# Hybrid encoder layer on one core: other buffers for the latent branch's operands, POOL for the preparation's copies

## The chip, the cores and the metric

The kernel runs on one core of one Trainium2 chip. The metric is device time in microseconds (us), the median of several executions; the profile is of one execution. The engines are TensorE (PE; its weight loads are listed as PEld), VectorE (DVE), ScalarE (ACT), GpSimd (POOL) and the queue of SyncE (SP), which issues most transfers.

## The reference, cut to what matters

One encoder layer in float32 over 2 x 256 tokens of width 1024. After an RMS norm, one wide projection feeds three branches, each with a silu gate and its own projection (br) to 1024 columns; the three are gated, added, projected by w_out and added to x, and a last norm follows.

```python
o_fwd = _gdn_chunked(q, k, v, g[:, :, 0], beta[:, :, 0])          # branch A, 8 heads, both directions
o_gdn = _rmsnorm(o_fwd + o_bwd, gdn_norm_gain) * silu(z_gdn)
o_mla = _blocked_attention(q_full, k_full, v_mla, scale) * silu(z_mla)   # branch B, "latent"
o_mem = (softmax(qx @ km.T) @ vm) * silu(z_mem)                   # branch C, memory tokens
merged = (gates[0] * (o_gdn @ w_br_gdn) + gates[1] * (o_mla @ w_br_mla)
          + gates[2] * (o_mem @ w_br_mem))
return x + merged @ w_out
```

Branch A is a gated delta rule. Within blocks of 32 tokens it needs the inverse of a triangular matrix (I + L) for every head, direction and block.

## The kernel before, in words

All large products are done in three passes of rounded operands (hi x hi, lo x hi, hi x lo). `gemm` (L231) does one tile of 128 outputs by 512 tokens: 8 blocks of the input x 3 passes = 24 matmuls, which the planner counts at 0.234 us each. `weight` (L196) loads the tile's 512 KB of weights on SP into one of two buffers, rounds them on ScalarE (wh, L207) and takes the rest on VectorE (wl, L211). `split` (L216) does the same for an operand: hi on ScalarE (L219), lo on VectorE (L223). Activations on chip are tiles of 128 x 512.

There are three stages. `front` does the memory and latent attention and writes the latent branch's 8 gated operands to DRAM (d_xa). `middle` does the 8 heads of branch A. `back` does the projection of branch A (bg, needs all heads' normed outputs xg; head 7's operand is used in the last 3 of a tile's 24 matmuls), then the output.

**The order in the middle.** `weave` (L1515) writes PE's order by hand from a plan. Several chains of small steps each yield (PE time, delay until their next step); in between, `products` takes single matmuls from a list of filling (`self.fill`, L1365 to L1372): projections, gates, and at its end the memory branch (`branch_mem`, a gate tile g and 12 products be for each of 8 tiles) and the latent branch's projection (`branch`, tiles bm). The first entry that `can` (L1502) allows is taken; where none is allowed, the plan's clock jumps. Only PE's order is fixed so. The other engines' and queues' instructions are put in order by a scheduler that goes by priority and its own estimate of readiness; `issue_after` keeps an instruction behind another on its engine.

**A head's chain.** Its decays e and values are loaded (L912 to L919; head h waits until head h-3 has given its output), its keys split into kh, kl (L959, L961) and multiplied (kk, L971). A solve (`gdn_solve`, two lanes: even and odd heads) follows, in links about 6.5 planned us apart: p (L1022, reads t32), yp (L1047, reads y32), then twice u (L1078), xs (L1088), us (L1097), with x (L1068) between the two rounds. ScalarE copies the results (u2 L1080, ub L1083 and L1100). The output o (L1121) reads ub; so (L1137) sums squares 11 planned us later (13 for head 7), and after a trip through DRAM the normed operand xg is split (L1153, L219, L223).

**The preparation** (`gdn_prep`, once for heads 0 to 3 and once for 4 to 7) inverts all blocks at once on VectorE: 31 steps of two instructions, then ScalarE reorders tt into ts (L873), VectorE transposes ts and tt into o1 and o2 (L876, L878), and ScalarE copies parts of them into t32 (four of 32 partitions, L891) and y32 (L895, L899).

**The latent operands** are read back from d_xa in six parts (`load_xa`, L1570) into tiles that something else has given up, and split (`split_xa`, L1581). Tags are shared storage: na is a head's masked keys (3 buffers), y0 and y1 the two lanes' block matrices, ub a head's result (2), y32 as above (2). A split is placed at the earliest XAT = 14 planned us after its load, except for part 5. Tile 7 of `branch_mem` is held until part 5 has been asked for (L1511), and no `branch` starts until all eight operands are split (L1513).

Of the kernel before, what the change touches and what calls it, by code (L numbers as in the profile page):

```python
# [7 lines left out]
F32 = mybir.dt.float32  # L8
F32R = mybir.dt.float32r
AF = mybir.ActivationFunctionType  # L10
# [3 lines left out]
P = 128  # L14
# [4 lines left out]
XAT = 14.0  # L19
# [136 lines left out]
class Layer:  # L156
# [74 lines left out]
    def gemm(self, src, nk, xs, name, m=P, ps=None):  # L231

        nc = self.nc
        hi, lo = self.weight(src, nk * m, name)
        ps = self.ps_gm("gm_" + name) if ps is None else ps
        n = 0
        order = [(p, k) for p in ((hi, 0), (hi, 1), (lo, 0)) for k in range(nk)]
        last = {"bm": 6, "bg": 7, "qm": 4}.get(name[:2])
        if last:

            order.sort(key=lambda o: o[1] >= last)
        for (a, j), k in order:
            nc.tensor.matmul(ps[:m], a[:, k * m:(k + 1) * m], xs[k][j],  # L243
                             start=n == 0, stop=n == 3 * nk - 1)
            n += 1
            yield 0.234
        return ps
# [526 lines left out]
    def gdn_prep(self, g):  # L774
# [4 lines left out]
        nc, c = self.nc, self.c  # L779
# [33 lines left out]
        with self.tc.high_priority(offset=0 if g else 900):  # L813
            for h in range(4):
                for s in range(2):
                    for cc in range(2):
                        w = h * 4 + s * 2 + cc
                        for a in range(4):
                            t = slice(cc * P + 32 * a, cc * P + 32 * a + 32)
# [28 lines left out]
        for d in range(2):  # L848
            t = self.tb(f"nd{g}{d}").rearrange("p (w i) -> p w i", i=32)
# [14 lines left out]
        tt, tms = self.tt, self.pb.tile([P, 4, 256], F32, tag="blk", bufs=3, name=f"tm{g}")  # L864
# [5 lines left out]
            nc.vector.tensor_tensor(tt[:, m:, 0:m], tt[:, m:, 0:m], t3, op=ALU.add)  # L870
            yield 0.0, 1.2
        ts = self.pb.tile([P, 32, 32], F32, tag="blk", bufs=3, name=f"ts{g}")
        nc.scalar.activation(ts, tt.rearrange("p r c -> p c r"), AF.Copy)  # L873
        yield 0.0, 4.0
        o1 = self.pb.tile([P, 32, 32], F32, tag="blk", bufs=3, name=f"o1{g}")
        nc.vector.transpose(out=o1.rearrange("p i j -> p (i j)"), in_=ts.rearrange("p i j -> p (i j)"))  # L876
        o2 = self.pb.tile([P, 32, 32], F32, tag="blk", bufs=3, name=f"o2{g}")
# [6 lines left out]
        t32 = self.pg.tile([P, 16, 32], F32, tag="t32", bufs=2, name=f"t32{g}")  # L884

        y32 = self.pg.tile([P, 32, 32], F32, tag="y32", bufs=2, name=f"y32{g}")
        for a in range(4):
            r = slice(32 * a, 32 * a + 32)
            d = a % 2
            with self.tc.issue_after(self.wround):  # L890
                nc.scalar.activation(t32[r], (o2 if d else o1)[r, :, 16 * d:16 * d + 16].rearrange("p i u -> p u i"),  # L891
                                     AF.Copy)
            yield 0.0, 4.5 if g else 2.8
        with self.tc.issue_after(self.wround):
            nc.scalar.activation(y32[:, 0:16], o2[:, :, 0:16].rearrange("p i u -> p u i"), AF.Copy)  # L895
        yield 0.0, 4.5 if g else 2.8
        for q in range(2):
            with self.tc.issue_after(self.wround):
                nc.scalar.activation(y32[:, 16 + q:32:2], o1[:, :, 17 - q:32:2].rearrange("p i u -> p u i"), AF.Copy)  # L899
            yield 0.0, 4.5 if g else 2.8  # L900
        self.ready[g] = self.now + 4
        return t32, y32, cc

# [598 lines left out]
    def can(self, f, *a):  # L1502

        if f == self.load_xa:
            return (3 in self.ub and self.pr[1], 5 in self.ub and 7 in self.hd, 6 in self.ub and 7 in self.hd,
                    7 in self.started, self.out > 6 and 7 in self.started, 7 in self.ub)[a[0]]
        if f == self.split_x:
            return self.now > self.xe_at
        if f == self.split_xa:
            return self.now > self.xa_at.get(a[0], 1e9)  # L1510
        if f == self.branch_mem and a[0] == 7:  # L1511
            return 5 in self.xa_raw
        return f != self.branch or None not in self.xa  # L1513

    def weave(self, *chains):  # L1515
# [53 lines left out]

    def load_xa(self, part):  # L1570

        lo, tags = ((0, ("y32",)), (1, ("na",)), (2, ("na", "y0")), (4, ("y32",)), (5, ("ub",)), (6, ("na", "y1")))[part]
        ts = [self.pg.tile([P, 2, 512], F32R, tag=t, bufs={"na": 3, "y0": 1, "y1": 1}.get(t, 2), name=f"xa{f}")
              for f, t in enumerate(tags, lo)]
        for f, t in enumerate(ts, lo):
            self.nc.sync.dma_start(t[:, 1].bitcast(F32), self.d_xa[:, f])
        self.xa_at[part] = self.now + XAT if part < 5 else self.now
        self.xa_raw[part] = ts, lo
        yield 0.0

    def split_xa(self, part):  # L1581
        ts, lo = self.xa_raw[part]
        with self.tc.issue_after(self.wround):
            for f, t in enumerate(ts, lo):
                self.xa[f] = t[:, 0], t[:, 1]
                self.split(t[:, 1].bitcast(F32), t[:, 0], t[:, 1], 0.5)
        yield 0.0


# [22 lines left out]
```

## Time and profile before

| | us |
|---|---|
| median of 3 executions (878.02 to 880.48) | 880.07 |
| the profiled execution | 877.71 |
| its span, first to last instruction | 875.9 |
| PE busy in it | 855.2 (98%) |
| VectorE, ScalarE, POOL busy | 564.1, 472.5, 120.1 |

Busy time says how long an engine had an instruction, not how late it got it. PE is nearly always busy, so what there is to read are the few stretches where it is not, and the granted clock there (1.00 is TensorE's full speed). A bracket behind an instruction gives the idle time before it on its engine and what ended it.

### The profile page before, as it was taken

How to read it: one execution, taken by the hardware profiler on the slowest of the kernel's cores; microseconds unless marked ns; L12 is line 12 of the kernel's file. 1: busy time of each engine (PE TensorE's matmuls, PEld its weight loads, DVE VectorE, ACT ScalarE, POOL GpSimd, SP SyncE). 2: the span in 40 equal slices, each digit the busy share in tenths (PEclk: the TensorE clock that was granted, in tenths of full speed). 3: DMA queues.
4: the chain of work that ended last, by engine and by line, in shares of the span. 5: the costliest groups of instructions: out<-in, count | busy, mean ns of one | idle time of the engine just before them, and what ended most of it. 6: DMA issues, size and time to landing. Idle time of an engine off the chain costs nothing.

```text
span 875.9 us, 13248 instructions
## 1 busy us (share of the span) xinstructions
PE 855.2 (98%) x4854; PEld 705.2 (81%) x4854; DVE 564.1 (64%) x1013; ACT 472.5 (54%) x915; POOL 120.1 (14%) x119
## 2 busy tenths in 40 slices
PE   8999998999999999999999989999999989999997
PEld 7878887878888888887888878888888878888886
DVE  7776458866989765547889967584654443335643
ACT  7655455554654565676675677666464532222232
POOL 0200111000100000141101211311110001432121
PEclk9999999999999999999999999999999989999999
DMA  9322212442235324373323455535533435465332
GB/s 330 127 91 79 90 67 64 133 140 76 83 112 160 120 90 147 115 216 109 105 90 126 127 156 168 160 111 159 169 123 95 164 123 201 161 221 183 120 97 96
DMA packets 50865, 116.10 MB, mean 133 GB/s; under 512 B 7152, under 2 KB 12656, under 8 KB 50800
## 3 DMA queue, kind: packets, MB, share of 16 engines
q1 hardware_dynamic: 44896, 104.51, 37.4%
q10 hardware_dynamic: 5904, 10.75, 3.5%
q8 instruction: 38, 0.62, 0.3%
q14 instruction: 27, 0.22, 0.1%
HBM read 95.09 MB, written 16.99 MB: 128 GB/s over the span
## 4 chain that ended last, share of the span: by engine, by line
PE 92%; ACT 3%; DVE 2%; DMA 2%; issue 1%; POOL 0%; POOLq 0%; DVEq 0%; ACTq 0%; SPq 0%
PE gm_g L243 16%; PE gm_qkv L243 14%; PE gm_z L243 7%; PE gm_bm L243 5%; PE gm_bg L243 5%; PE gm_za L243 5%; PE y L1256 4%; PE vm L396 3%; PE o L1121 3%; PE gm_be L243 3%; PE gm_qm L243 3%; PE gm_km L243 3%; PE kk L971 2%; PE s_a L305 2%; PE gm_cq L243 2%; PE gm_qn L243 2%
## 5 line engine op out<-in xcount | busy, mean ns | idle before, releaser
L742 DVE SCALAR_TENSOR_TENSOR kq<-cz,prm,kq 128x510 f32<-128x510 f32 (+1 forms) x64 | 47.8, 747 | 13.3 <-ACT kq L735 12.6
L243 PE MATMUL gm_g<-hh,wh_g 128*128 128x512 f32 x192 | 52.0, 405 | 0.6 <-ACT cz L733 0.6
L243 PE MATMUL gm_g<-hh,wl_g 128*128 128x512 f32 x192 | 51.8, 400 | 0.0
L243 PE MATMUL gm_qkv<-hh,wl_qkv 128*128 128x512 f32 x192 | 51.6, 399 | 0.0
L243 PE MATMUL gm_g<-hl,wh_g 128*128 128x512 f32 x192 | 50.4, 398 | 0.0
L243 PE MATMUL gm_qkv<-hh,wh_qkv 128*128 128x512 f32 x192 | 50.4, 399 | 0.0
L243 PE MATMUL gm_qkv<-hl,wh_qkv 128*128 128x512 f32 x192 | 49.7, 396 | 0.0
L211 DVE TENSOR_TENSOR wl_qkv<-wr_qkv,wh_qkv 128x1024 fp32r<-128x1024 f32 x24 | 30.0, 1249 | 26.7 <-ACT wh_qkv L207 12.2
L211 DVE TENSOR_TENSOR wl_g<-wr_g,wh_g 128x1024 fp32r<-128x1024 f32 x24 | 29.5, 1229 | 21.6 <-ACT wh_g L207 11.2
L243 PEld LDWEIGHTS gm_qkv<-hl,wh_qkv 128*128 128x128 f32 x192 | 35.8, 188 | 8.3
L243 PEld LDWEIGHTS gm_g<-hh,wh_g 128*128 128x128 f32 x192 | 35.4, 191 | 8.4 <-ACT cz L733 1.0
L243 PEld LDWEIGHTS gm_g<-hl,wh_g 128*128 128x128 f32 x192 | 35.5, 188 | 7.9
L243 PEld LDWEIGHTS gm_g<-hh,wl_g 128*128 128x128 f32 x192 | 35.2, 188 | 7.4
L243 PEld LDWEIGHTS gm_qkv<-hh,wl_qkv 128*128 128x128 f32 x192 | 35.2, 188 | 7.4
L243 PEld LDWEIGHTS gm_qkv<-hh,wh_qkv 128*128 128x128 f32 x192 | 35.1, 188 | 7.5
L1256 PE MATMUL y<-wh_wo,mh 128*128 128x512 f32 (+1 forms) x144 | 40.0, 370 | 0.0
L1226 POOL TENSOR_TENSOR mg<-mg,lg 128x512 f32<-128x512 f32 x16 | 28.0, 1750 | 57.2 <-DVE lg L1225 52.7
L207 ACT ACTIVATE wh_qkv<-wr_qkv 128x1024 fp32r<-128x1024 f32 x24 | 25.3, 1055 | 19.1 <-PE gm_qkv L243 4.7
L207 ACT ACTIVATE wh_g<-wr_g 128x1024 fp32r<-128x1024 f32 x24 | 25.3, 1056 | 17.1 <-PE gm_g L243 6.0
L961 POOL TENSOR_TENSOR kl<-kq,kh 128x512 fp32r<-128x512 f32 x16 | 22.1, 1386 | 81.3 <-ACT kh L959 81.2
L243 PE MATMUL gm_bm<-xa,wh_bm 128*128 128x512 f32 x128 | 32.4, 395 | 0.0
L243 PE MATMUL gm_bg<-xg,wh_bg 128*128 128x512 f32 x128 | 32.4, 394 | 0.0
(433 smaller groups left out, 2200.8 us busy)
## 6 DMA issues: line engine op xcount, KB each, us to landing
wr_qkv<-in_w_dram SPq DMA_DIRECT2D x24, 512.0 KB
wr_g<-in_w_dram SPq DMA_DIRECT2D x24, 512.0 KB
e<-d_r SPq DMA_DIRECT2D x64, 96.0 KB
wr_z<-in_w_dram SPq DMA_DIRECT2D x12, 512.0 KB
wr_za<-in_w_dram SPq DMA_DIRECT2D x8, 512.0 KB
d_g<-gt_g ACTq DMA_DIRECT2D x16, 256.0 KB
wr_bm<-in_w_dram SPq DMA_DIRECT2D x8, 512.0 KB
lg<-d_g SPq DMA_DIRECT2D x16, 256.0 KB
```

What stands on the lines that cost most here:

```text
L207: self.wround = nc.scalar.activation(hi[:, :n], raw[:, :n], AF.Copy).ins
L211: d = eng.tensor_tensor(lo[:, :n], raw[:, :n], hi[:, :n].bitcast(F32), op=ALU.subtract)
L243: nc.tensor.matmul(ps[:m], a[:, k * m:(k + 1) * m], xs[k][j], start=n == 0, stop=n == 3 * nk - 1)
L305: nc.tensor.matmul(sp[:, qb * 256:(qb + 1) * 256], a, b, start=j == 0, stop=j == n - 1)
L396: nc.tensor.matmul(vps[tb], ms[k][a][:, t], b[:, :512], start=k == 0 and i == 0, stop=k == 7 and i == 2)
L742: nc.vector.scalar_tensor_tensor(ys, zs, self.cw[:, f, m:m + 1], ys, ALU.mult, ALU.add)
L961: nc.gpsimd.tensor_tensor(lo, src, hi.bitcast(F32), op=ALU.subtract)
L971: nc.tensor.matmul(ps, a[:, k], b, start=i == 0, stop=i == 2)
L1121: nc.tensor.matmul(out, ub[:, d, s, cp], rhs, start=n == 0, stop=n == 3)
L1226: nc.gpsimd.tensor_tensor(self.merged[d], self.merged[d], gt, op=ALU.add)
L1256: nc.tensor.matmul(ps, xs[2 * j + q][a][:, t], b[:, q * 512 + c0:q * 512 + c1], start=j == 0 and n == 0, stop=j == 3 and n == 5)
```

## The change

The transfers of the latent operands go to other tiles: operands 3 and 4 to the keys' tiles (kh and kl), 5 to y32, 6 to two tiles of decays (e), 7 to two of t32; 0, 1 and 2 as before to y32 and na. Parts are grouped anew, the conditions under which the plan asks for them are others, all parts are split 14 planned us after their load at the earliest, and tile 7 of the memory branch is no longer held. In a bm tile the products with operands 5 to 7 instead of 6 and 7 come last. The preparation's eight copies of each pass are made by POOL, without being kept behind a weight's rounding, and the plan counts 2.8 us after each of the last seven in both passes (before: 4.5 in the second).

```diff
--- before.py
+++ after.py
@@ -235,7 +235,7 @@
         ps = self.ps_gm("gm_" + name) if ps is None else ps
         n = 0
         order = [(p, k) for p in ((hi, 0), (hi, 1), (lo, 0)) for k in range(nk)]
-        last = {"bm": 6, "bg": 7, "qm": 4}.get(name[:2])
+        last = {"bm": 5, "bg": 7, "qm": 4}.get(name[:2])
         if last:
 
             order.sort(key=lambda o: o[1] >= last)
@@ -870,7 +870,7 @@
             nc.vector.tensor_tensor(tt[:, m:, 0:m], tt[:, m:, 0:m], t3, op=ALU.add)
             yield 0.0, 1.2
         ts = self.pb.tile([P, 32, 32], F32, tag="blk", bufs=3, name=f"ts{g}")
-        nc.scalar.activation(ts, tt.rearrange("p r c -> p c r"), AF.Copy)
+        nc.gpsimd.tensor_copy(out=ts, in_=tt.rearrange("p r c -> p c r"))
         yield 0.0, 4.0
         o1 = self.pb.tile([P, 32, 32], F32, tag="blk", bufs=3, name=f"o1{g}")
         nc.vector.transpose(out=o1.rearrange("p i j -> p (i j)"), in_=ts.rearrange("p i j -> p (i j)"))
@@ -887,17 +887,13 @@
         for a in range(4):
             r = slice(32 * a, 32 * a + 32)
             d = a % 2
-            with self.tc.issue_after(self.wround):
-                nc.scalar.activation(t32[r], (o2 if d else o1)[r, :, 16 * d:16 * d + 16].rearrange("p i u -> p u i"),
-                                     AF.Copy)
-            yield 0.0, 4.5 if g else 2.8
-        with self.tc.issue_after(self.wround):
-            nc.scalar.activation(y32[:, 0:16], o2[:, :, 0:16].rearrange("p i u -> p u i"), AF.Copy)
-        yield 0.0, 4.5 if g else 2.8
+            nc.gpsimd.tensor_copy(out=t32[r], in_=(o2 if d else o1)[r, :, 16 * d:16 * d + 16].rearrange("p i u -> p u i"))
+            yield 0.0, 2.8
+        nc.gpsimd.tensor_copy(out=y32[:, 0:16], in_=o2[:, :, 0:16].rearrange("p i u -> p u i"))
+        yield 0.0, 2.8
         for q in range(2):
-            with self.tc.issue_after(self.wround):
-                nc.scalar.activation(y32[:, 16 + q:32:2], o1[:, :, 17 - q:32:2].rearrange("p i u -> p u i"), AF.Copy)
-            yield 0.0, 4.5 if g else 2.8
+            nc.gpsimd.tensor_copy(out=y32[:, 16 + q:32:2], in_=o1[:, :, 17 - q:32:2].rearrange("p i u -> p u i"))
+            yield 0.0, 2.8
         self.ready[g] = self.now + 4
         return t32, y32, cc
 
@@ -1502,14 +1498,12 @@
     def can(self, f, *a):
 
         if f == self.load_xa:
-            return (3 in self.ub and self.pr[1], 5 in self.ub and 7 in self.hd, 6 in self.ub and 7 in self.hd,
-                    7 in self.started, self.out > 6 and 7 in self.started, 7 in self.ub)[a[0]]
+            return (3 in self.ub and self.pr[1], 4 in self.ub and 7 in self.hd, 5 in self.ub and 7 in self.hd,
+                    7 in self.hd, self.out > 5, 7 in self.started)[a[0]]
         if f == self.split_x:
             return self.now > self.xe_at
         if f == self.split_xa:
             return self.now > self.xa_at.get(a[0], 1e9)
-        if f == self.branch_mem and a[0] == 7:
-            return 5 in self.xa_raw
         return f != self.branch or None not in self.xa
 
     def weave(self, *chains):
@@ -1569,21 +1563,26 @@
 
     def load_xa(self, part):
 
-        lo, tags = ((0, ("y32",)), (1, ("na",)), (2, ("na", "y0")), (4, ("y32",)), (5, ("ub",)), (6, ("na", "y1")))[part]
-        ts = [self.pg.tile([P, 2, 512], F32R, tag=t, bufs={"na": 3, "y0": 1, "y1": 1}.get(t, 2), name=f"xa{f}")
-              for f, t in enumerate(tags, lo)]
-        for f, t in enumerate(ts, lo):
-            self.nc.sync.dma_start(t[:, 1].bitcast(F32), self.d_xa[:, f])
-        self.xa_at[part] = self.now + XAT if part < 5 else self.now
-        self.xa_raw[part] = ts, lo
+        parts = (((0, "y32"),), ((1, "na"),), ((2, "na"),), ((3, "kh", "kl"), (4, "kh", "kl")), ((6, "e", "e"),),
+                 ((5, "y32"), (7, "t32", "t32")))[part]
+        bufs = {"na": 3, "e": 6}
+        self.xa_raw[part] = {}
+        for f, *tags in parts:
+            if len(tags) == 1:
+                t = self.pg.tile([P, 2, 512], F32R, tag=tags[0], bufs=bufs.get(tags[0], 2), name=f"xa{f}")
+                hi, lo = t[:, 0], t[:, 1]
+            else:
+                hi, lo = (self.pg.tile([P, 512], F32R, tag=t, bufs=bufs.get(t, 2), name=f"xa{f}") for t in tags)
+            self.nc.sync.dma_start(lo.bitcast(F32), self.d_xa[:, f])
+            self.xa_raw[part][f] = hi, lo
+        self.xa_at[part] = self.now + XAT
         yield 0.0
 
     def split_xa(self, part):
-        ts, lo = self.xa_raw[part]
         with self.tc.issue_after(self.wround):
-            for f, t in enumerate(ts, lo):
-                self.xa[f] = t[:, 0], t[:, 1]
-                self.split(t[:, 1].bitcast(F32), t[:, 0], t[:, 1], 0.5)
+            for f, (hi, lo) in self.xa_raw[part].items():
+                self.xa[f] = hi, lo
+                self.split(lo.bitcast(F32), hi, lo, 0.5)
         yield 0.0
```

## Rows read from the trace of the kernel before

**Rows 1.** The page: span, and section 1 (busy us, share of the span, instructions).

```profile
span 875.9 us, 13248 instructions
...
PE 855.2 (98%) x4854; PEld 705.2 (81%) x4854; DVE 564.1 (64%) x1013; ACT 472.5 (54%) x915; POOL 120.1 (14%) x119
```

**Rows 2.** Busy time by stretches (us, then each engine's busy us, PE's clock, DMA).

```profile
375.00:400.00 25.00, 25.00 (x109) 20.14 (x108) 12.24 (x16) 17.31 (x27) 9.74 (x17) 1.00 0.66 187
505.00:530.00 25.00, 21.99 (x138) 18.35 (x140) 17.27 (x33) 19.30 (x32) 5.31 (x7) 1.00 0.57 177
711.40:726.40 15.00, 11.15 (x48) 9.62 (x48) 6.51 (x13) 4.37 (x10) 1.01 (x1) 0.66 0.46 162
...
715.00:725.00 10.00, 8.01 (x29) 6.92 (x30) 2.35 (x6) 3.56 (x8) 1.01 (x1) 0.50 0.34 116
```

**Rows 3.** Chain of waits, 495 to 535 (start us, us, what).

```profile
503.87 2.13 ACT ts L873
...
514.04 1.07 ACT y L895
...
515.13 0.39 ACT ub L1100
...
515.56 2.45 PE o L1121 x14
```

**Rows 4.** Timeline, 503 to 521 (start us, us, engine line op out<-in).

```profile
504.57 0.61 PE L1097 MATMUL us<-w,y 128*128 128x128 f32 x4
...
518.36 1.30 POOL L961 TENSOR_TENSOR kl<-kq,kh 128x512 fp32r<-128x512 f32 x1 [14.84 <-ACT kh L959]
...
520.74 0.48 PE L971 MATMUL kk<-kh 128*128 128x512 f32 x1
```

**Rows 5.** Chain of waits, 676 to 780.

```profile
677.17 0.79 PE so L1137 x8
...
680.16 0.89 PE x L1068 x8
...
694.85 0.44 PE xs L1088 x4
...
701.82 0.44 PE us L1097 x4
...
708.77 2.63 PE o L1121 x16
...
711.42 4.83 DMA xa<-d_xa
...
726.40 4.88 PE gm_g L243 x21
731.28 2.81 PE gm_be L243 x12
...
740.25 39.54 PE gm_bm L243 x169
```

**Rows 6.** Timeline, 681 to 717: issue and split of the latent operands.

```profile
682.21 0.86 SPq L1576 DMA_DIRECT2D xa<-d_xa  x2
...
716.33 0.63 ACT L219 ACTIVATE xa<-xa 128x512 fp32r<-128x512 f32 x1 [3.52 <-DMA xa<-d_xa]
```

**Rows 7.** POOL's memset of line 1450 (ns min/median/max).

```profile
L1450 POOL MEMSET y<- x2: 955/956/957, 374.0 to 375.2; 128x1024 f32 x2
```

**Rows 8.** Timeline, 780 to 787: VectorE's and POOL's two-input instructions.

```profile
780.49 1.22 DVE L211 TENSOR_TENSOR wl_bg<-wr_bg,wh_bg 128x1024 fp32r<-128x1024 f32 x1
...
786.25 1.29 POOL L1226 TENSOR_TENSOR mg<-mg,lg 128x512 f32<-128x512 f32 x1 [3.39 <-DVE lg L1225]
786.28 2.35 DVE L211 TENSOR_TENSOR wl_bg<-wr_bg,wh_bg 128x1024 fp32r<-128x1024 f32 x1
```

**Rows 9.** Timeline, 738 to 754: head 7's sums and its normed operand.

```profile
739.30 0.95 PE L1137 MATMUL so<-cst,sq 128*128 128x1 f32 x8
...
753.22 0.69 DVE L223 SCALAR_TENSOR_TENSOR xg<-og,xg 128x512 fp32r<-128x512 f32 x1 [0.70 <-ACT xg L219]
```

## The prediction

> **What bounds the kernel now.** I read the page first: PE is busy for 855.2 of 875.9 us [rows 1]. The products are a fixed amount of work, so the change can only win time in which PE stands still or runs at a lower clock. The second view is the table of busy time by stretches of 10 us, to find such places; two fall out of those after 380 us, and [rows 2] show them cut to size: 505 to 530 (21.99 of 25.00, clock 1.00) and 711.4 to 726.4 (11.15 of 15.00, granted clock 0.66). The third view is the chain of waits through each, and the fourth the timeline, for what stood in front of the late instruction.
>
> Hole A, at 512 to 515.5: 25.00 - 21.99 = 3.01 us without a product. The chain [rows 3] leaves PE and runs through ScalarE: the copy ts (2.13 us), the copies of t32 and y32 (the last 1.07), then ub of L1100, and only then the output product o of head 1. That ub comes from the product us at 504.57 [rows 4], so it was ready to be copied at about 505.2 and was copied at 515.13, behind the preparation's blocks. The planner counts 6.5 us from us to o.
>
> Hole B, from 711.4: after the output product of head 6 there is nothing left to fill PE with. The last gate and memory product (branch_mem 7) is held until part 5 of the latent operands is loaded, and the latent products (bm) until all are split. So head 7's last links run bare, and ScalarE even holds u of head 7 behind a split that waits for its transfer: the chain has 4.83 us of DMA xa<-d_xa [rows 5], ScalarE stood 3.52 us for it [rows 6]. From 715 to 725 the granted clock is 0.50 (1.2 of 2.4 GHz) [rows 2], after a stretch in which PE did little, and the output product of head 7 runs through all of it.
>
> What B costs: from 711.4 to 726.4 PE computes x, u, so, xs, us, three products of a gate and one o. At full clock [rows 5] these take 0.89 + 0.44 + 0.79 + 0.44 + 0.44 + 0.70 (3 of 21 in 4.88) + 2.63 = 6.33 us (u, xs and us are alike). 15.0 - 6.33 = 8.67 us are lost.
>
> **The change, part by part.**
> *Copies to POOL.* Eight ScalarE copies leave each of the two passes. In the second, L1100 would then find ScalarE free at about 506, o starts at 512 as placed, and hole A goes: -3.0. The first pass falls where PE stands at 25.00 of 25.00, 375 to 400 [rows 2]: nothing to win. The planner's gaps of 4.5 become 2.8, so it thinks the blocks ready some 12 us sooner; but head 4 waits for its keys and decays, whose loads hang on the output of head 1, not for these: 0.
>
> What POOL pays: the trace shows no copy on POOL. Nearest rows: a memset of 128x1024 in 0.96 us [rows 7], which reads nothing, as the lower end; a subtraction of 128x512 with two inputs in 1.30 [rows 4] as the upper (2.6 for 1024). A copy has one input, so I take the middle: 1.8 for ts, 0.9 per 512 elements, of which the other seven hold six. That makes 7.2 us for the second pass (2.8 + 1.0 = 3.8 to 10.4). VectorE's transpose now waits for POOL's ts instead of ScalarE's; at 1.8 against 2.13 that is level, at worst 0.5 later. Queued behind on POOL is kl of head 3 (1.30), which the product kk at 520.74 needs [rows 4], 517.7 once A is gone. With ts from 503.9, 1.3 for the transpose and the copies behind it, POOL is done at 503.9 + 1.3 + 7.2 = 512.4 (516 at the upper end), kl 1.3 later: in time either way. In the first pass the cover is as wide (POOL 9.74 busy of 25).
>
> What VectorE pays: at 786.25 POOL starts an addition of 1.29 us, VectorE's subtraction starts 0.03 later and takes 2.35, where the same one takes 1.22 started first [rows 8]: one was held for the other's whole length. So a POOL copy can hold a VectorE instruction with two inputs in SBUF by up to its own length: 0 to 10.4 us of VectorE in the second pass. VectorE is busy for 17.27 of the 25 us there [rows 2], which leaves 7.7. I take 0.5 us of PE time for it; ends 0 and 3.0.
> The Trainium skill states this as a rule (SBUF — State Buffer, "Who interferes with whom"): GpSimd and VectorE share a port pair, and a VectorE instruction with two SBUF inputs contends with a GpSimd instruction that reads SBUF. By that rule all sixteen copies contend, which speaks against the change; the trace agrees, with 2.35 us against 1.22.
>
> *Operands into other buffers.* The same eight transfers, splits and bytes; only when they go changes. Before, each transfer was issued when its buffer came free: two at 682.21 [rows 6], right behind x of head 6, and the last ones from 711.4 on, behind the output of head 6 and x and us of head 7. Now operands 3 and 4 go into the keys' tiles, read by head 7 before its solve, 6 into the decays of head 5, 7 into t32 and 5 into y32, both read by head 7's first two steps; 1 and 2 stay in na, and 2 is free after x of head 6 at 680.16 + 0.89 [rows 5]. The last part is asked for when head 7 is started, at its first u. Links lie 6.97 us apart where there is filling (xs at 694.85, us at 701.82 [rows 5]), so that u is three links before x at 711.4: 690. The split is placed 14 planned us later (XAT), at 704, before 711. On SP the late issues move to before 690, between the weights; none is added. On ScalarE a split is 0.63 us [rows 6]; moved among the weight roundings I count it at 0, since the lead of the weights covers it (without that cover: rival 3).
>
> *Head 7's links covered.* branch_mem 7 is no longer held: 24 + 12 products, 5.6 + 2.81 us, and behind it 8 x 24 of bm, 169 of which take 39.54 [rows 5]. From x to o there is then need of four links, some 28 us, and there are over 50 of filling. Hole B goes whole: -8.7. Grouping bm's products at operand 5 instead of 6 changes their order only: 0.
> What comes late next: head 7's output. x at 708.4 gives o at 736, so at 752, and its normed operand took 14.6 us from so (739.30 to 753.91) [rows 9]: 767. The last stage starts at 779.79 - 11.7 = 768.1 and uses operand 7 in its last three products of 24, 4.9 us later: covered by 6 us.
>
> **Sum.** -3.0 - 8.7 + 0.5 = -11.2 us. The profiled execution took 877.71 (span 875.9 and 1.8 around it), which would become 866.5; it stands 2.36 below the median of 880.07, so against the median I say 868.9. Differences within 0.3% (2.6 us, about the spread of the three runs) cannot be told from none.
>
> **Rivals.**
> 1. *POOL gives A back.* The copies hold VectorE for their full 10.4 us against 7.7 of slack, 2.7 us show at PE as weights that come late, and A's 3.0 are gone: 880.07 - 8.7 = 871.4. For it: the 2.35 us. Against: most VectorE work here has an input in PSUM, and POOL is held as often as it holds. 0.14. It is the rule of the Trainium skill just named, at its hardest.
> 2. *Only branch_mem 7 covers.* If the last split is placed after 711, bm cannot start; 8.4 us cover x and u, the last links run bare, and about half of B stays: 880.07 - 2.5 - 4.4 = 873.2. For it: the margin is 704 against 711. 0.10.
> 3. *Slower: ScalarE held by early splits.* The splits now stand among the weight roundings of 660 to 705. If the scheduler puts one on ScalarE when its transfer is only issued, ScalarE stands for up to 4.83 us, and roundings and ub behind it come late, as at 716.33, which is part of how B came to cost 8.7. One such stall leaves a gain; two (17.4) outweigh 11.2 and give 886.3. Against: the filling is there, and in 375 to 400 PE stays full with ScalarE busy 17.31 of 25 us [rows 2]. 0.04.
> 4. *Nothing moves in the tail*, because a buffer taken is freed no sooner than the old one; only A goes: 880.07 - 2.5 = 877.6, within 0.3%. 0.04.
>
> **How the numbers follow.** My forecast has 0.68. The range runs from 865.5 (no cost on VectorE, and the profiled run's lower base in part) to 874.5, over rivals 1 and 2; rivals 3 and 4 are left out. Faster: 0.68 + 0.14 + 0.10 = 0.92; same 0.04; slower 0.04.
>
> **What would show it.** Right: no stretch under 10.00 for PE at 505 to 530 and at 700 to 745, granted clock 1.00 in both; all transfers of xa issued by about 692; bm products between x and o of head 7; the last stage (bg) starting near 768; copies of some 1 us on POOL. Rival 1 shows as PE waiting for wl or for kk behind POOL; rival 2 as bare links at 715 to 730; rival 3 as ScalarE idle before xa for over 4 us with PE idle beside it. I am wrong if o of head 1 still waits, or if a hole of over 3 us opens elsewhere.

## The result and the profile after

| | before | after |
|---|---|---|
| median, on the same chip (range, 4 executions each) | 879.05 (875.69 to 880.48) | 867.22 (866.09 to 867.57) |
| the profiled execution, and its span | 877.71, 875.9 | 867.27, 865.5 |
| VectorE, ScalarE, POOL busy | 564.1, 472.5, 120.1 | 574.6, 455.9, 143.2 |

The ratio is 0.9869 [0.9844, 0.9894]: 1.3% faster. From median to median that is -11.8 us, between the profiled executions -10.4; forecast were -11.2.

The page of the kernel after, against [rows 1]:

```profile
span 865.5 us, 13255 instructions
...
PE 851.6 (98%) x4854; PEld 703.0 (81%) x4854; DVE 574.6 (66%) x1013; ACT 455.9 (53%) x899; POOL 143.2 (17%) x135
```

Sixteen instructions went from ScalarE to POOL (915 to 899, 119 to 135). VectorE has the same 1013 instructions and is busy 10.5 us longer. With the loads alone (below) it is busy 566.7 us, so 2.6 of the 10.5 come with the loads and some 8 with the copies on POOL, which hold it (rows below). Lines behind the preparation lie 4 lower than before. Busy time by stretches, against [rows 2] (us, then the busy us of PE, PEld, VectorE, ScalarE and POOL, the granted clock, DMA):

```profile
505.00:530.00 25.00, 25.00 (x161) 21.17 (x160) 22.53 (x36) 12.77 (x27) 16.72 (x15) 1.00 0.58 180
375.00:400.00 25.00, 25.00 (x111) 20.25 (x111) 13.50 (x13) 11.66 (x21) 19.38 (x25) 1.00 0.72 208
700.00:745.00 45.00, 45.00 (x223) 37.63 (x222) 19.59 (x27) 14.35 (x23) 7.60 (x4) 1.00 0.55 184
711.40:726.40 15.00, 15.00 (x74) 12.42 (x74) 6.02 (x11) 4.65 (x8) 1.01 (x1) 1.00 0.58 191
140.00:145.00 5.00, 4.24 (x14) 3.51 (x15) 4.42 (x14) 2.03 (x6) 0.56 (x1) 0.66 0.00 2
```

Both holes are gone: 25.00 of 25.00 where 21.99 stood, 15.00 of 15.00 at clock 1.00 where 11.15 at 0.66 stood. The last row lies in the front stage, which the change doesn't touch; it comes back below.

The chain of waits of the kernel after, 699 to 800, against [rows 5] (start us, us, what):

```profile
707.42 2.62 PE o L1117 x16
710.04 0.89 PE x L1064 x8
710.93 5.12 PE gm_g L243 x22
...
717.45 0.44 PE u L1074 x4
...
719.29 2.80 PE gm_bm L243 x12
...
731.35 0.45 PE us L1093 x4
...
739.26 2.62 PE o L1117 x16
...
769.38 30.80 PE gm_bg L243 x132
```

Nothing but PE stands in it. Between x and o of head 7 lies filling: tile 7 of the memory branch (gm_g and gm_be, the latter left out here) until 719.29, then the latent products gm_bm. The links are longer apart than before, about 7 us each, and that costs nothing, since PE does other work between them.

The timeline of the kernel after around 505 to 518 (start us, us, engine line op out<-in, idle before):

```profile
499.52 0.68 DVE L744 SCALAR_TENSOR_TENSOR kq<-cz,kq 128x512 f32<-128x512 f32 x1
...
505.14 1.23 DVE L211 TENSOR_TENSOR wl_z<-wr_z,wh_z 128x1024 fp32r<-128x1024 f32 x1
505.29 3.03 POOL L873 COPY ts<-tt 128x1024 f32<-128x1024 f32 x1 [0.34 <-DVE tt L870]
505.94 0.61 PE L1093 MATMUL us<-w,y 128*128 128x128 f32 x4
506.28 2.60 DVE L744 SCALAR_TENSOR_TENSOR vf<-cz,vf 128x512 f32<-128x512 f32 x1
508.06 0.78 ACT L1096 ACTIVATE ub<-us 64x256 f32<-64x256 f32 x2
510.43 2.66 POOL L890 COPY t<-o 32x512 f32<-32x512 f32 x2 [2.11 <-DVE o L876]
512.00 2.17 DVE L211 TENSOR_TENSOR wl_qkv<-wr_qkv,wh_qkv 128x1024 fp32r<-128x1024 f32 x1
513.15 2.11 POOL L895 COPY y<-o 128x256 f32<-128x256 f32 x2
513.33 2.78 PE L1117 MATMUL o<-e,ub 128*128 128x256 f32 x16
515.31 2.65 POOL L890 COPY t<-o 32x512 f32<-32x512 f32 x2
518.02 1.09 POOL L892 COPY y<-o 128x512 f32<-128x512 f32 x1
519.08 1.29 POOL L957 TENSOR_TENSOR kl<-kq,kh 128x512 fp32r<-128x512 f32 x1
```

ub (L1096, before L1100) now follows its product by 1.5 us where it took 10, and o starts without a wait. The price is to be seen too. POOL's five rows of copies sum to 3.03 + 2.66 + 2.11 + 2.65 + 1.09 = 11.5 us. In the first pass, on POOL's timeline of the same execution, they take 9.4 us:

```profile
298.25 2.40 POOL L873 COPY ts<-tt 128x1024 f32<-128x1024 f32 x1 [71.09 <-DVE tt L870]
...
375.02 4.57 POOL L890 COPY t<-o 32x512 f32<-32x512 f32 x4 [18.94 <-PE oa L340]
379.65 1.14 POOL L892 COPY y<-o 128x512 f32<-128x512 f32 x1
380.72 1.27 POOL L895 COPY y<-o 128x256 f32<-128x256 f32 x2
```

The instruction of L744 (two inputs of 128x512) took 0.68 at 499.52 and 2.60 when it began behind POOL's copy ts; it ended 0.56 us after that copy. The rule of the Trainium skill named in the prediction (SBUF — State Buffer, "Who interferes with whom") is borne out by these rows, 2.60 against 0.68.

### The profile page after: what moved, and what is told of

It is laid out like the page before. It is cut to its first block, busy times and chain, and to the rows that moved or that the text cites. A ratio compares the mean times of both kernels' runs of the same rounds, so it can differ in the third digit from the quotient of the medians.

```text
span 865.5 us, 13255 instructions
## 1 busy us (share of the span) xinstructions
PE 851.6 (98%) x4854; PEld 703.0 (81%) x4854; DVE 574.6 (66%) x1013; ACT 455.9 (53%) x899; POOL 143.2 (17%) x135
## 4 chain that ended last, share of the span: by engine, by line
PE 94%; DVE 2%; DMA 2%; ACT 1%; issue 1%; POOL 0%; POOLq 0%; DVEq 0%; ACTq 0%; SPq 0%
PE gm_g L243 16%; PE gm_qkv L243 14%; PE gm_z L243 8%; PE gm_bm L243 5%; PE gm_bg L243 5%; PE gm_za L243 5%; PE y L1252 5%; PE gm_be L243 3%; PE gm_qm L243 3%; PE gm_km L243 3%; PE kk L967 3%; PE o L1117 2%; PE s_a L305 2%; PE vm L396 2%; PE gm_cq L243 2%; PE gm_qn L243 2%
## 5 line engine op out<-in xcount | busy, mean ns | idle before, releaser
L211 DVE TENSOR_TENSOR wl_qkv<-wr_qkv,wh_qkv 128x1024 fp32r<-128x1024 f32 x24 | 31.4, 1308 | 27.7 <-PE gm_qkv L243 10.5
```

The source lines that it names most:

```text
L211: d = eng.tensor_tensor(lo[:, :n], raw[:, :n], hi[:, :n].bitcast(F32), op=ALU.subtract)
```

## The experiments

The theory was that the two holes are separate: POOL's copies close A, the loads and the lifted hold close B, and neither touches the other. The first four kernels take the change apart.

**The copies alone** (before, with POOL's copies and their yields of 2.8 us as in the diff; loads as before).

> The kernel before with the sixteen copies on POOL and nothing else. Theory: hole A (3.0 us at 512) closes and hole B (8.7 us from 711) stays, so the time is about 3.0 below the kernel before, ratio 0.9966; PE 25.00 of 25.00 at 505 to 530 and a wait of PE near 711 to 722 as before. Rival (POOL holds VectorE, A is given back): ratio 1.000, PE below 25.00 somewhere in 505 to 530, waiting for a weight's wl or for kk.

Measured: 874.46 (873.87 to 876.59), ratio 0.9946 [0.9926, 0.9966]. Its stretches, then two pieces of its chain from 704:

```profile
505.00:530.00 25.00, 25.00 (x159) 21.13 (x159) 21.39 (x35) 14.32 (x32) 16.61 (x16) 1.00 0.67 186
700.00:745.00 45.00, 40.16 (x191) 33.48 (x190) 18.57 (x29) 13.68 (x22) 5.22 (x4) 0.92 0.49 166
```

```profile
708.14 5.17 DMA xa<-d_xa
...
719.27 3.24 PE o L1117 x16
```

A is closed; B stands as before, with the same transfer in the chain. The profiled span fell by 3.9 us, of which 3.0 are A's idle time. The median fell by 5.4, more than expected; the section on the hardware says what may be behind that.

**The loads alone** (after, with ScalarE's copies and their yields of before).

> The kernel after with the copies back on ScalarE, so only the operands' new buffers, their conditions and the free branch_mem 7. Theory: hole B closes, hole A stays, 8.7 us below the kernel before, ratio 0.990; PE 21.99 of 25 at 505 to 530 with o of head 1 waiting 3.0 us for ub, 15.00 of 15.00 at 711 to 726. Rival (the two holes are one late chain, and either part mends both): about 867, ratio 0.987.

Measured: 870.93 (869.62 to 872.12), ratio 0.9901 [0.9871, 0.9932], span 867.8, which is -8.1. Its stretches, then the one wait of PE in 505 to 530 (us in total, times, longest):

```profile
505.00:530.00 25.00, 21.98 (x116) 18.32 (x114) 17.20 (x34) 19.22 (x30) 5.31 (x7) 1.00 0.55 178
700.00:745.00 45.00, 45.00 (x224) 37.63 (x222) 20.75 (x28) 13.77 (x22) 6.70 (x4) 1.00 0.56 189
```

```profile
PE o L1121 <- ACT ub L1100: 3.0, 1, 3.0
```

The mirror image: B closed, A as in [rows 2]. The parts don't need each other. By their medians they gain 5.4 and 8.9, together more than the whole's 11.8; the intervals (3.0 to 6.5 and 6.0 to 11.3) are too wide to add them up.

**Only the hold lifted.**

```diff
--- before.py
-        if f == self.branch_mem and a[0] == 7:
-            return 5 in self.xa_raw
```

> The kernel before with branch_mem 7 no longer held, operands in their old buffers. Theory: 8.4 us of products slip between x and u of head 7, the later links still run bare because the latent products wait for operands that come with head 7's own results; about half of B stays, 4 to 5 us below the kernel before, ratio 0.995; the granted clock falls again after 720. Rival (the hold alone made hole B): 8.7 below, ratio 0.990. Rival (the operands alone made it): no change, ratio 1.000.

Measured: 874.66 (873.67 to 877.3), ratio 0.9945 [0.9929, 0.9961]. Stretches, PE's waits in 700 to 745, and two pieces of the chain (start us, us, what):

```profile
505.00:530.00 25.00, 21.85 (x103) 18.01 (x102) 16.29 (x32) 19.25 (x32) 5.29 (x7) 0.93 0.55 175
700.00:745.00 45.00, 42.43 (x212) 34.77 (x211) 21.97 (x32) 16.17 (x27) 5.42 (x3) 1.00 0.58 187
```

```profile
PE gm_bm L243 <- ACT xa L219: 1.3, 1, 1.3
PE us L1097 <- DVE w L1092: 1.2, 1, 1.2
```

```profile
705.57 0.45 PE us L1097 x4
...
776.48 23.56 PE gm_bg L243 x101
```

45.00 - 42.43 = 2.57 us of idle are left, at full clock; the expected fall of the clock did not come. What B costs in all can be read from the chains, as the time from the last us of head 6 to the first bg, with the same products in between: 75.9 us in the kernel before (703.88 to 779.79), 70.9 here, 67.3 in the kernel after (702.06 to 769.38). So these two lines of the change bring 5.0 of 8.6 us, and the loads are needed for the other 3.6. The profiled span fell by 3.3 only; in this execution the stretch with A ran at clock 0.93.

**The hold put back** (after, with those two lines, and bm's products grouped at operand 6 again).

> The kernel after with branch_mem 7 held again until part 5 is asked for, and with bm's products grouped at operand 6 again. Theory: part 5 is asked for about 20 us before that tile's turn, and the grouping only changes an order, so nothing changes: ratio to the kernel before 0.987 as the kernel after, PE full at 700 to 745. Rival (the free tile is what closes the hole): some 4 us above the kernel after, ratio 0.991.

Measured: 866.63 (866.14 to 866.92), ratio 0.9851 [0.9819, 0.9883], PE full in both stretches. With the early loads, part 5 has been asked for (680.01 in the kernel after) long before tile 7 is wanted (710.93), so the hold holds nothing. The loads give the whole cover with or without the hold; lifting the hold without them gives 5.0 of 8.6 us.

**Every POOL copy made twice** (after; each of the sixteen copies is issued a second time, with the same result). This doubles the copies, whose cost is disputed.

> The kernel after with every POOL copy of the preparation made twice in a row (the second writes the same again), which doubles the time in which POOL can hold VectorE: some 23 us instead of 11.5 in the second pass. VectorE is busy for 22.5 of 25 us at 505 to 530 in the kernel after, 5.3 more than before. Theory: that first hold fitted into VectorE's spare time with about 2.5 us left, and a second one does not, so PE waits 2 to 4 us for weights or for head 3's operands near 505 to 530: ratio 0.990 to 0.992. Rival (the weights' lead covers any such hold): the time of the kernel after, 0.986, PE full.

Measured: 868.88 (868.0 to 869.08), ratio 0.9882 [0.9862, 0.9902]; the kernel after, run again, took 866.89 (866.18 to 867.51). Its stretches, then two rows of VectorE's timeline:

```profile
370.00:380.00 10.00, 8.34 (x35) 6.39 (x34) 3.86 (x6) 4.23 (x11) 5.82 (x6) 0.83 0.64 180
505.00:530.00 25.00, 25.00 (x163) 21.27 (x162) 22.95 (x37) 12.84 (x25) 19.73 (x17) 1.00 0.55 158
```

```profile
370.48 1.23 DVE L211 TENSOR_TENSOR wl_g<-wr_g,wh_g 128x1024 fp32r<-128x1024 f32 x1 [1.95 <-PE gm_za L243]
371.62 0.16 DVE L322 RECIPROCAL rs_a<-sm_a 128x2 f32<-128x2 f32 x1
```

My expectation failed: in the second pass even twice the copies take no product's place. They take 22.1 us and last until 541.1; PE is full at 530 to 545 as well. VectorE is busy 7.7 us longer in all than in the kernel after (582.3 against 574.6).

The 2 us more lie at 370 to 383. PE has 0.6 us less there than the 8.95 of the kernel after, and the 24 products behind the wait take 6.64 us instead of 5.58, with the clock at 0.50 from 376 to 378. No copy ran beside that wait: POOL stood idle from 353.36 to 373.99. On VectorE the latent attention's rs_a stood behind the rounding of a weight; in the kernel after, run again, it went first (rs_a at 370.30, wl_g at 370.59), and ph_a and PE's products follow from rs_a. That points to an instruction's place once more, and not to held time; why the order differs was not tested.

**The place instead of the engine.** If A is a matter of what stands in front of ub, ScalarE can keep the copies so long as they come behind it. A first try put the second pass's copies behind the newest ub known when they were given out.

> The loads-only kernel with the second pass's copies still on ScalarE, but each kept behind the newest ub copy of L1100 by an explicit order. Theory: hole A is the place of the copies in ScalarE's order and not their time; ub of head 1 goes first, o starts as placed, the hole closes and the time is that of the kernel after, ratio 0.986, with PE 25.00 at 505 to 530. Rival (ScalarE has too much to do there): the hole stays or moves to another wait for ScalarE, ratio 0.990 as loads only.

Measured: 868.67 (867.82 to 870.55), ratio 0.9885 [0.9864, 0.9906]. The edit missed: ub of head 1 was not yet given out, so the copies were tied to an older one, and ub still came at 514.95. PE waited 2.1 us for it. This run decides nothing. The second also holds the copies in the plan until that ub exists:

```diff
--- after.py
+        while g and 1 not in self.ub:
+            yield 0.0, 1.0
...
-            nc.gpsimd.tensor_copy(out=t32[r], ...)
+            with self.tc.issue_after(self.lub if g else self.wround):
+                nc.scalar.activation(t32[r], ..., AF.Copy)
...
+                self.lub = nc.scalar.activation(ub[t, d, :, cp], u3[t], AF.Copy).ins
```

> The loads-only kernel with the second pass's t32 and y32 copies on ScalarE, not given out before the plan has given out head 1's last ub, and kept behind that ub. Unlike the run before it, where the order named an older ub, this puts ub of head 1 in front of seven of the eight copies. Theory: hole A closes without POOL, since what made it is the place in ScalarE's order; PE 25.00 at 505 to 530, ratio to the kernel before 0.986 as the kernel after. Rival (ScalarE's time is too short there): the wait moves to another consumer of ScalarE within 20 us, ratio 0.989 to 0.990.

Measured: 866.11 (865.94 to 866.31), ratio 0.9838 [0.9817, 0.986]. Its stretch and ScalarE's timeline:

```profile
505.00:530.00 25.00, 25.00 (x159) 21.10 (x158) 18.01 (x34) 20.44 (x36) 6.74 (x8) 1.00 0.58 186
```

```profile
503.89 2.12 ACT L873 ACTIVATE ts<-tt 128x1024 f32<-128x1024 f32 x1
...
507.63 0.78 ACT L1102 ACTIVATE ub<-us 64x256 f32<-64x256 f32 x2
...
510.59 0.77 ACT L1102 ACTIVATE ub<-us 64x256 f32<-64x256 f32 x2
511.26 4.53 ACT L893 ACTIVATE t<-o 32x512 f32<-32x512 f32 x4
```

A closes without POOL, while ScalarE does more in this stretch (20.44 us) than before (19.30 in [rows 2]). So ScalarE was never short of time there: the order was wrong, and moving the copies to POOL is one way of taking them out of ub's way. The plan's gaps of 4.5 us are those of the kernel before, so the shorter gaps aren't needed either. VectorE is busy 18.01 us instead of 22.53: vf and wl_qkv take 0.68 and 1.22 us again, and wl_z falls before this stretch.

**The latent products given out late** (after, with part 5's split at the earliest 45 planned us after its load instead of 14), to price rival 2.

> The kernel after with the last part's split placed 45 planned us after its load instead of 14, so at some 735, 16 us after the end of branch_mem 7. Theory: as in my second rival, the latent products cannot start, the links xs and us of head 7 run bare, and 3 to 5 us come back over the kernel after, ratio to the kernel before 0.990 to 0.992, with PE short of 10.00 at 719 to 735. Rival (the filling of branch_mem 7 alone closes the hole): no change against the kernel after.

Measured: 867.73 (867.59 to 869.13), ratio 0.9856 [0.983, 0.9881].

```profile
700.00:745.00 45.00, 43.74 (x219) 36.35 (x218) 19.97 (x29) 14.24 (x23) 7.50 (x5) 1.00 0.51 169
```

```profile
717.37 0.44 PE u L1074 x4
...
722.93 2.45 PE o L1117 x14
725.38 11.20 PE gm_bm L243 x48
```

On ScalarE the split stayed where it was (706.51; in the kernel after 706.59), since only PE's order is written by the plan. But gm_bm begins at 725.38 instead of 719.29, and the links behind u run bare as rival 2 has it. It costs 45.00 - 43.74 = 1.26 us of idle, at full clock. From the last us of head 6 to the first bg it takes 69.1 us (701.99 to 771.07), 1.8 more than the kernel after; rival 2 had 4.4.

**Other places with idle time.** In the front stage PE has 17.47 of 20 us at 130 to 150; 1.5 of the 2.5 us are a wait for the scaling of a memory head's softmax on VectorE. Two kernels move that scaling to ScalarE, for all heads (`if True:` in place of `if name[0] == "a":`) or for head 3 alone (`or name[1] == "3"`).

> The kernel after with the two scalings of each memory head's softmax on ScalarE, as the latent heads have them, instead of VectorE. In the kernel after PE loses 2.5 us at 130 to 150, 1.5 of it for these scalings, with VectorE busy 9.96 of 10 and ScalarE 5.2. Theory: PE waits less there, 1 to 2.5 us below the kernel after, ratio to the kernel before 0.984. Rival (the softmax chain is as long on ScalarE, or another wait of the chain takes its place): no change against the kernel after, 0.986.

> The kernel after with the scalings of memory head 3 alone on ScalarE; heads 0 to 2 stay on VectorE, so that no new wait comes at 80 to 90, as it did with all four. Theory: 1 to 1.5 us of PE's waits at 130 to 150 go and none comes, 866 us, ratio to the kernel before 0.985. Rival (the wait for the scalings is replaced by others of the same softmax chain): no change against the kernel after.

Measured: 868.23 (867.35 to 869.01), ratio 0.9877 [0.9859, 0.9895], and 865.94 (865.15 to 867.37), ratio 0.9838 [0.9814, 0.9861]. With all heads the stretch has 18.49, but PE waits anew at 80 to 90 (8.83 of 10.00, for cqs on ScalarE) and at 620 to 630 (9.17). With head 3 alone it has 17.58: the idle time stayed.

**The kernel after again, beside the two best together.**

> The kernel after once more, beside the next kernel on the same chip. Both theories: 866 to 867 us, ratio to the kernel before about 0.986.

> The operands' new buffers, the second pass's copies on ScalarE behind ub of head 1, and the scalings of memory head 3 on ScalarE. Theory: neither hole, POOL free of copies, VectorE held less; 0.5 to 1.5 us below the kernel after beside it, most of it within what a measurement can tell. Rival (the differences of about 1 us between the kernels without holes are scatter of the executions): the same time as the kernel after.

Measured: 866.89 (866.18 to 867.51), ratio 0.9855 [0.9834, 0.9876], and 866.52 (865.12 to 868.26), ratio 0.9845 [0.9824, 0.9866]. They can't be told apart, and the intervals of the two edits run singly overlap with these. Where both holes are closed and no new wait was opened, the medians lie between 865.94 and 867.22; no version shown here beats the kernel after beyond doubt.

## Why the prediction was right

**Hole A, -3.0: right, cause and size.** o of head 1 stood behind copies in ScalarE's order [rows 3]. The loads alone leave 21.98 of 25.00 and a wait of 3.0 us, the copies alone leave none, and the kernel with the copies behind ub shows that their place was the cause.

**Hole B, -8.7: right.** The stretch now holds 15.00 us of work at full clock. From the last us of head 6 to the first bg the kernel after takes 8.6 us less, and so do the loads alone, whose span fell by 8.1. What I had not seen is how it splits: lifting the hold on tile 7 gives 5.0 of the 8.6, though with the new loads the lift is not needed.

**POOL's copies, "7.2 us for the second pass (2.8 + 1.0 = 3.8 to 10.4)": mis-sized.** They took 11.5, beyond the upper end. Two steps failed. The middle between a memset and a subtraction was too low: in the first pass the copies take 9.4, those behind ts with little of VectorE beside them. And I let POOL hold VectorE but not VectorE hold POOL, which the other 2.1 point to. The trace before has such a case next to [rows 8]: POOL's addition at 780.65, begun 0.16 behind VectorE's subtraction, took 2.21 instead of 1.29. The transpose, which I had "at worst 0.5 later", began 3.84 us after the start of ts instead of 2.15. That none of this mattered was luck, since a third step was wrong as well: I took kl of [rows 4] for what "the product kk at 520.74 needs". In the kernel after those kk run at 518.8 to 520.1, before kl at 519.08 is done; kl's user is the kk at 542. POOL had over 20 us of cover.

**VectorE, +0.5: no cost shown.** The hold is real: vf, wl_qkv and xg beside the copies take 2.60, 2.17 and 1.12 us instead of 0.69, 1.22 and 0.69, 3.3 more in all. VectorE's busy time at 505 to 530 rose by 5.3, from 17.27 to 22.53; the rest is in the main wl_z (1.23), which now falls into this stretch. That fits into the 7.7 us of slack: no product waited for it, nor in this pass with the copies doubled. This also answers rival 1: its mechanism is there, its price is not.

**The buffers and the splits: right, with the margin mis-stated.** I wrote transfers "issued by about 692" and "the margin is 704 against 711". SP issued the last two at 680.01, the last splits ran from 706.59 on ScalarE to 709.5 on VectorE, and ScalarE stood for no transfer, so rival 3 is out. But tile 7 of the memory branch fills PE until 719.29, so bm is wanted 8 us later than I said: from the plan's 704 the margin is about 15 us, not 7, and from the end of the splits about 10.

**Rival 2, "about half of B stays" (4.4): overpriced.** The kernel with late latent products lost 1.8 us. With only the hold lifted, where the transfers come late too, 3.6 of 8.6 stayed. I halved a cost of which only 15.00 - 11.15 = 3.85 us were idle; the other 4.8 were the low clock, which neither of these two profiles shows. That it takes the whole hole, with the split waiting in front of u, is my reading and was not tested.

**What came late next.** The links came 1 to 3 us after my dates (u 717.45 for 715, o 739.26 for 736, so 754.96 for 752, bg 769.38 for 768.1), in part because this execution lost 1.5 us at 140 to 150. Head 7's normed operand was ready at 767.8, and bg used it about 4.9 us after its start (21 products), without a wait.

**The sum.** The profiled span fell by 10.4 instead of 11.2; with the 1.5 us at 140 to 150 returned it would be 11.9, and without the 0.5 for VectorE my sum is 11.7.

## What to carry to other kernels

When an instruction that PE waits for is late, look at what stands in front of it on its engine before looking at that engine's busy time: the copies' place cost 3 us while ScalarE had time enough, and putting them behind ub or on POOL cures it equally. For the last of several chains, see that filling is still allowed: operands loaded early into buffers already read, and no hold that outlives its reason. Before pricing contention on an engine off the critical path, compare the held time with its slack in that stretch; here 3.3 us of holding against 7.7 us of slack cost nothing.

## What the runs showed of the hardware

**The same idle time does not always bring the same clock.** At 140 to 145 the front stage has the same idle in both kernels; the kernel before in its profiled execution:

```profile
140.00:145.00 5.00, 4.23 (x20) 3.47 (x21) 4.78 (x15) 2.03 (x6) 0.57 (x1) 1.00 0.00 2
```

Clock 1.00 with 4.23 us busy there, 0.66 with 4.24 in the kernel after (its row stands above; 0.50 from 141 to 144), and from there to 150 the latter falls 1.5 us behind. Likewise hole A, with the clock at 1.00 over 505 to 530 in the kernel before and in the loads alone, at 0.93 with the hold lifted, where A is wider by 0.14 us, and at 0.93 with the copies tied to an older ub, where it is narrower (22.94 busy). The medians fit to that: the copies alone gain 5.4 where the idle is 3.0, and the kernel before spreads from 876.5 to 881.96 over 15 executions, with a mean clock of 0.995 in the fastest and 0.988 in the slowest, while the kernel after, run again, spreads over 1.3 in four, all at 0.999. I read it as an idle hole costing its width in every execution and a lower clock in some; that the spread comes from these two holes was argued from such rows and not shown execution by execution.

**POOL copies these blocks about as fast as ScalarE**: four t32 blocks in 4.57 us against 4.53, 128x512 in 1.14 against 1.14, ts in 2.40 against 2.12. The difference is what runs beside them. In the second pass ts took 3.03: it began 0.15 us behind VectorE's wl_z, which ran at its usual 1.23, and vf, which began behind ts, took 2.60 for 0.68. In these rows the one that began second was the one that took longer.
